# Two unused tiles that shift where a kernel's matmul operands start in on-chip memory

## The chip, the cores and the metric

The kernel runs on one core of one Trainium2 chip. The metric is the device time of one execution in microseconds, given as the median of several runs. Beside it stands one profiled execution, whose trace is read below: PE is the matrix engine (TensorE), PEld its weight loads, DVE the vector engine, ACT the scalar engine, POOL the general engine, SP the engine that issues the DMAs. SBUF is the on-chip memory of 128 partitions, PSUM the memory into which matmuls accumulate.

## The reference

One encoder block in float32 on x of shape (1, 512, 2048): RMSNorm, one input projection, windowed attention beside a chunked gate, one output projection, then a gated MLP with a depthwise convolution of width 3.

```python
z = rmsnorm(x, norm1_g) @ w_in                    # 2048 -> 3584
attn = windowed_gqa(q, k, v, attn_sink)           # 8 heads, 2 kv heads, |t-s| <= 128
gm = chunked_spatial_gating(zg, ...)              # u * (ws @ v + b), 8 groups, chunks of 128
x = x + concat(rmsnorm(attn), rmsnorm(gm)) @ w_out        # 2048 -> 2048
a = rmsnorm(x, norm2_g) @ w_up                    # 2048 -> 11264
g, u = split(conv3(a) + conv_b)
x = x + (silu(g) * u) @ w_down                    # 5632 -> 2048
return rmsnorm(x, final_g)
```

## The kernel before

**Numbers in two halves.** Every matrix operand is held as two float32r tiles, a rounded high part and the remainder. ACT makes the high part (a cast, L76, L89, L446), DVE the remainder (a subtraction, L77, L90, L447). `mm3` (L80 to L83) multiplies two such pairs with three matmuls into one PSUM tile: L81 is high times high, L82 high weights times the low moving part, L83 low weights times the high moving part. In each matmul one operand is *stationary* (128 columns, loaded into PE by an LDWEIGHTS of its own) and the other is *moving* (512 columns as a rule, streamed through PE). There are 8776 of each in the trace; nearly all of the work is 8124 matmuls with 512 moving columns.

**Stages, in order of time.** `g`, `va`, `u` and `vg_ps` are the input projection, with the attention's small matmuls (`sc`, `pt`, `o`) between. `gv` is the chunk gate. `pj` is the output projection, in two halves: in the first the stationary operand is the attention result `atsh`, `atsl`, in the second the gate result `gm..s_h`, `gm..s_l`; the moving operand is in both halves the converted weight `hi_o`, `lo_o`. `up` is the MLP's up-projection (4224 matmuls), interleaved with `dp`, the down-projection in a form with seven block products instead of eight (1680 matmuls, in runs of 12). `dn` is the last group of the down-projection.

**Where the operands lie.** Tiles come from pools, which the framework places one behind the other in SBUF. In order of address: `const` (columns of constants, `ones`, `ident` and others), `big` (64 slots of 2048 bytes a partition: activations `x_h`, `h_h`, `gm..s_h`, `al`, `dl_h`), `tmp`, `small`, then the weight pool `wp`, later `wq` in its place (`st_`, `hi_`, `lo_` tiles of 4096 bytes), and last `oct`, later `raw`, `acp` and `afp` (`atsh`, `afs`, `af`). Since slots and tiles of the larger pools are multiples of 512 bytes, every operand of one pool starts at the same place modulo 256 bytes, which is set by the sizes of the small tiles ahead of it.

**What sets the order.** Each engine runs its own stream in program order, and the framework's semaphores hold an instruction until its operands are ready. Weights are loaded by SP's DMAs of 512 KB, three (front) or six (MLP) tiles ahead.

## Time and profile before

| | |
|---|---|
| median of three runs | 1995.55 us (1995.38 to 1996.44) |
| profiled execution, its own time | 1995.75 us |
| span in its trace, first to last instruction | 1994.0 us |
| PE busy | 1971.3 us, 99% of the span |
| DVE, ACT, POOL busy | 63%, 35%, 3% |
| granted clock of PE, mean | 0.995 of full |

In the trace the duration of a matmul is modelled and longer than the distance to the next one, since matmuls overlap in PE's pipeline. What counts for the time is the distance from one start to the next. The timeline prints starts to 0.01 us, so that distance is best read over many matmuls in a row: last start less first start, over the number of steps.

### The profile page before, as it was taken

How to read it: one execution, taken by the hardware profiler on the slowest of the kernel's cores; microseconds unless marked ns; L12 is line 12 of the kernel's file. 1: busy time of each engine (PE TensorE's matmuls, PEld its weight loads, DVE VectorE, ACT ScalarE, POOL GpSimd, SP SyncE). 2: the span in 40 equal slices, each digit the busy share in tenths (PEclk: the TensorE clock that was granted, in tenths of full speed). 3: DMA queues.
4: the chain of work that ended last, by engine and by line, in shares of the span. 5: the costliest groups of instructions: out<-in, count | busy, mean ns of one | idle time of the engine just before them, and what ended most of it. 6: DMA issues, size and time to landing. Idle time of an engine off the chain costs nothing.

```text
span 1994.0 us, 21954 instructions
## 1 busy us (share of the span) xinstructions
PE 1971.3 (99%) x8776; PEld 1605.1 (80%) x8776; DVE 1261.5 (63%) x1692; ACT 694.6 (35%) x915; POOL 58.1 (3%) x64
## 2 busy tenths in 40 slices
PE   9999999999999999999999999999999999999988
PEld 7887788888878888888888888888888888888866
DVE  7366563434444767667676676667766766758667
ACT  6243442322332333333233342333333333333243
POOL 5001100100000000000000000000000000000000
PEclk9999999999999999999999999999999999999989
DMA  6222232522132222232223322332232222232222
GB/s 219 85 74 66 74 114 85 169 99 91 53 148 84 95 95 95 95 117 85 95 96 115 107 85 96 106 106 95 86 108 103 97 94 104 93 119 85 95 100 102
DMA packets 59575, 201.07 MB, mean 101 GB/s; under 512 B 6864, under 2 KB 7120, under 8 KB 59472
## 3 DMA queue, kind: packets, MB, share of 16 engines
q1 hardware_dynamic: 59472, 199.67, 29.0%
q8 instruction: 68, 1.11, 0.2%
q14 instruction: 35, 0.29, 0.0%
HBM read 195.44 MB, written 4.19 MB: 100 GB/s over the span
## 4 chain that ended last, share of the span: by engine, by line
PE 96%; DVE 1%; issue 1%; DMA 1%; ACT 1%; POOL 0%; SPq 0%; ACTq 0%; DVEq 0%; POOLq 0%
PE up L83 16%; PE up L81 16%; PE up L82 16%; PE dp L82 6%; PE dp L83 6%; PE dp L81 6%; PE pj L81 3%; PE pj L83 3%; PE pj L82 3%; PE u L81 1%; PE vg_ps L83 1%; PE vg_ps L81 1%; PE vg_ps L82 1%; PE u L82 1%; PE u L83 1%; PE g L81 1%
## 5 line engine op out<-in xcount | busy, mean ns | idle before, releaser
L81 PE MATMUL up<-h_h,hi_u 128*128 128x512 f32 x1408 | 555.9, 395 | 2.5 <-ACT hi_u L446 2.5
L83 PE MATMUL up<-h_h,lo_u 128*128 128x512 f32 x1408 | 556.1, 395 | 0.2 <-DVE lo_u L447 0.2
L82 PE MATMUL up<-h_l,hi_u 128*128 128x512 f32 x1408 | 555.4, 394 | 0.0
L81 PEld LDWEIGHTS up<-h_h,hi_u 128*128 128x128 f32 x1408 | 264.4, 188 | 64.5 <-ACT hi_u L446 2.7
L83 PEld LDWEIGHTS up<-h_h,lo_u 128*128 128x128 f32 x1408 | 264.3, 188 | 64.1 <-DVE lo_u L447 0.6
L82 PEld LDWEIGHTS up<-h_l,hi_u 128*128 128x128 f32 x1408 | 264.4, 188 | 63.5
L446 ACT CAST hi_u<-st_u 128x1024 fp32r<-128x1024 f32 x176 | 185.0, 1051 | 323.2 <-PE dp L83 189.4
L447 DVE TENSOR_TENSOR lo_u<-st_u,hi_u 128x1024 fp32r<-128x1024 f32 x176 | 215.0, 1222 | 97.8 <-ACT hi_u L446 97.8
L447 DVE TENSOR_TENSOR lo_b<-st_d,hi_b 128x1024 fp32r<-128x1024 f32 x60 | 73.4, 1223 | 163.0 <-ACT hi_b L446 163.0
L447 DVE TENSOR_TENSOR lo_t<-st_d,hi_t 128x1024 fp32r<-128x1024 f32 x60 | 73.5, 1226 | 126.6 <-ACT hi_t L446 126.6
L545 DVE TENSOR_TENSOR x<-x,dp 128x512 f32<-128x512 f32 x200 | 136.3, 681 | 4.6 <-PE dp L83 2.7
L446 ACT CAST hi_b<-st_d 128x1024 fp32r<-128x1024 f32 x60 | 63.1, 1052 | 193.1 <-PE up L82 193.1
L446 ACT CAST hi_t<-st_d 128x1024 fp32r<-128x1024 f32 x60 | 63.2, 1053 | 174.4 <-PE up L82 174.4
L77 DVE TENSOR_TENSOR lo_i<-st_i,hi_i 128x1024 fp32r<-128x1024 f32 (+1 forms) x57 | 72.8, 1277 | 78.2 <-ACT hi_i L76 78.0
L473 ACT ACTIVATE c<-a,col 128x512 f32<-128x512 f32 x88 | 71.3, 810 | 117.3 <-DVE a L470 117.3
L76 ACT CAST hi_i<-st_i 128x1024 fp32r<-128x1024 f32 (+1 forms) x57 | 58.7, 1031 | 125.4 <-PE u L82 35.6
L77 DVE TENSOR_TENSOR lo_o<-st_o,hi_o 128x1024 fp32r<-128x1024 f32 x32 | 39.2, 1225 | 97.0 <-ACT hi_o L76 97.0
L82 PE MATMUL dp<-lo_t,afs 128*128 128x512 f32 x240 | 93.7, 390 | 0.0
L83 PE MATMUL dp<-hi_t,afs 128*128 128x512 f32 x240 | 93.6, 390 | 0.0
L81 PE MATMUL dp<-hi_t,afs 128*128 128x512 f32 x240 | 93.6, 390 | 0.0
L475 DVE SCALAR_TENSOR_TENSOR c<-a,col,c 128x511 f32<-128x511 f32 x88 | 66.0, 750 | 24.7 <-ACT c L473 24.5
L76 ACT CAST hi_o<-st_o 128x1024 fp32r<-128x1024 f32 x32 | 33.7, 1052 | 115.9 <-PE pj L83 90.6
(278 smaller groups left out, 3210.2 us busy)
## 6 DMA issues: line engine op xcount, KB each, us to landing
st_u<-in_w_up SPq DMA_DIRECT2D x176, 512.0 KB, 3.2
st_d<-in_w_down SPq DMA_DIRECT2D x80, 512.0 KB, 3.2
st_i<-in_w_in SPq DMA_DIRECT2D x55, 512.0 KB, 3.2
st_o<-in_w_out SPq DMA_DIRECT2D x32, 512.0 KB, 3.2
xg<-in_xT SPq DMA_DIRECT2D x16, 256.0 KB, 4.8
x<-in_x SPq DMA_DIRECT2D x16, 256.0 KB, 5.9
st_l<-in_w_down SPq DMA_DIRECT2D x8, 512.0 KB, 3.2
out<-x SPq DMA_DIRECT2D x16, 256.0 KB, 3.0
```

Of the source, the lines that this page charges most:

```text
L76: nc.scalar.copy(hi[:, cs], st[:, cs])
L77: nc.vector.tensor_tensor(lo[:, cs], st[:, cs], f(hi[:, cs]), op=ALU.subtract)
L81: nc.tensor.matmul(ps, a[0], b[0], start=start, stop=False, skip_group_check=free)
L82: nc.tensor.matmul(ps, a[0], b[1], start=False, stop=False, skip_group_check=free)
L83: nc.tensor.matmul(ps, a[1], b[0], start=False, stop=stop, skip_group_check=free)
L446: nc.scalar.copy(hi, st)
L447: nc.vector.tensor_tensor(lo, st, f(hi), op=ALU.subtract)
L473: nc.scalar.activation(t, a, AF.Identity, scale=w[1], bias=col[:, C_CB + j * 44 + i : C_CB + j * 44 + i + 1])
L475: nc.vector.scalar_tensor_tensor(t[:, 1:], a[:, : S - 1], w[0], t[:, 1:], op0=ALU.mult, op1=ALU.add)
L545: nc.vector.tensor_tensor(d, d, ps, op=ALU.add)
```

## The change

Two tiles are allocated that nothing writes or reads: one of 56 float32 (224 bytes a partition) as the first tile of `const`, and one of 16 float32 (64 bytes) in `tmp`, which has two buffers a tile and so grows by 128 bytes.

```diff
+    tmp.tile([P, 16], F32, tag="gap", name="gap")
+    const.tile([P, 56], F32, name="gap0")
     col = const.tile([P, N_COLS], F32, name="col")
     ones = const.tile([P, P], F32, name="ones")
```

The instructions of all five engines, their order and the semaphores that they wait for stay the same; line numbers behind L119 go up by two. What moves is the addresses. In the built programs, the start of each operand modulo 256 bytes is:

| pool | operands | before | after |
|---|---|---|---|
| `const` | `ones`, `ident` | 224 | 192 |
| `big` | `x_h`, `h_h`, `gm..s_h`, `al`, `dl_h`, `vah`, `k_h` | 32 | 0 |
| `wp`, `wq` | `hi_i`, `hi_o`, `hi_u`, `hi_b`, `hi_t` and their `lo_` | 160 | 0 |
| `oct`, `raw`, `afp` | `atsh`, `atsl`, `af`, `afs` | 160 | 0 |

Matmuls of 512 moving columns, by the start of the moving and of the stationary operand before:

| moving | stationary | count | which |
|---|---|---|---|
| 32 | 160 | 5088 | `up` 4224, `g` 480, `u` 384 |
| 160 | 32 | 768 | `vg_ps` 384, `pj` second half 384 |
| 160 | 160 | 2064 | `dp` 1680, `pj` first half 384 |
| 32 | 32 | 204 | `dn` 144, `o` 60 |

So 5856 of the 8124 have their two operands 128 bytes apart modulo 256, and 2268 have them at the same place. After the change all 8124 have both at 0. Of the 256-column matmuls, 192 (`va`) have 160 and 32, and 144 (`dn` 96, `sc` 48) have 32 and 32.

## Rows read from the trace of the kernel before

**Rows 1.** The page: PE's busy time; the chain that ended last, by engine.
```profile
PE 1971.3 (99%) x8776; PEld 1605.1 (80%) x8776; DVE 1261.5 (63%) x1692; ACT 694.6 (35%) x915; POOL 58.1 (3%) x64
...
PE 96%; DVE 1%; issue 1%; DMA 1%; ACT 1%; POOL 0%; SPq 0%; ACTq 0%; DVEq 0%; POOLq 0%
```
**Rows 2.** The page's costliest groups: an up group and a dp group.
```profile
L81 PE MATMUL up<-h_h,hi_u 128*128 128x512 f32 x1408 | 555.9, 395 | 2.5 <-ACT hi_u L446 2.5
...
L82 PE MATMUL dp<-lo_t,afs 128*128 128x512 f32 x240 | 93.7, 390 | 0.0
```
**Rows 3.** Timeline, PE, pj first half: start us, duration us, engine, line, operands.
```profile
376.21 0.39 PE L83 MATMUL pj<-hi_o,atsl 128*128 128x512 f32 x1
...
460.53 0.40 PE L83 MATMUL pj<-hi_o,atsl 128*128 128x512 f32 x1
```
**Rows 4.** Timeline, PE, pj second half.
```profile
480.02 0.40 PE L82 MATMUL pj<-lo_o,gm6s_h 128*128 128x512 f32 x1
...
483.50 0.40 PE L82 MATMUL pj<-lo_o,gm7s_h 128*128 128x512 f32 x1
```
**Rows 5.** Timeline, PE, one unbroken run of up.
```profile
774.56 0.40 PE L81 MATMUL up<-h_h,hi_u 128*128 128x512 f32 x1
...
790.88 0.40 PE L82 MATMUL up<-h_l,hi_u 128*128 128x512 f32 x1
791.12 0.39 PE L83 MATMUL up<-h_h,lo_u 128*128 128x512 f32 x1
```
**Rows 6.** Timeline, PE, one unbroken run of vg_ps.
```profile
209.72 0.40 PE L82 MATMUL vg_ps<-lo_i,x_h 128*128 128x512 f32 x1
...
225.58 0.40 PE L81 MATMUL vg_ps<-hi_i,x_h 128*128 128x512 f32 x1
```
**Rows 7.** Timeline, PE, dn at 512 columns, in the tail.
```profile
1963.85 0.39 PE L81 MATMUL dn<-dl_h,al 128*128 128x512 f32 x1
...
1965.89 0.39 PE L81 MATMUL dn<-dl_h,al 128*128 128x512 f32 x1
```
**Rows 8.** Timeline, PE, one run of 12 dp and the up behind it.
```profile
671.90 0.39 PE L81 MATMUL dp<-hi_t,afs 128*128 128x512 f32 x1
...
672.60 0.39 PE L81 MATMUL dp<-hi_t,afs 128*128 128x512 f32 x1
672.83 0.39 PE L82 MATMUL dp<-lo_t,afs 128*128 128x512 f32 x1
...
674.64 0.40 PE L81 MATMUL up<-h_h,hi_u 128*128 128x512 f32 x1
```
**Rows 9.** Tile va (duration min/median/max ns, first, last start); timeline, dn at 256 columns.
```profile
L81 PE MATMUL va<-hi_i,x_h x64: 279/281/285, 80.1 to 102.5; 128*128 128x256 f32 x64
...
1961.74 0.28 PE L81 MATMUL dn<-dl_h,al 128*128 128x256 f32 x1
...
1962.34 0.28 PE L83 MATMUL dn<-dl_h,al 128*128 128x256 f32 x1
```
**Rows 10.** Timeline, PE, first dn matmuls of the tail.
```profile
1938.37 0.63 PE L81 MATMUL dn<-dl_h,al 128*128 128x512 f32 x1
...
1941.79 0.63 PE L83 MATMUL dn<-dl_h,al 128*128 128x512 f32 x1
```
**Rows 11.** Busy time by stretch: head, MLP, tail.
```profile
core 0: us, PE busy (x) PEld busy (x) DVE busy (x) ACT busy (x) POOL busy (x), PEclk, DMA share, GB/s
0.00:43.00 43.00, 38.60 (x165) 30.77 (x165) 31.66 (x27) 30.16 (x44) 26.90 (x21) 1.00 0.66 230
...
560.00:1930.00 1370.00, 1368.44 (x5912) 1109.12 (x5912) 924.51 (x1119) 463.11 (x519) 0.00 (x0) 1.00 0.29 100
...
1938.00:1942.00 4.00, 4.00 (x11) 3.13 (x10) 2.31 (x4) 4.00 (x9) 0.00 (x0) 0.50 0.65 192
```
**Rows 12.** Waits: waiter <- releaser: us in total, times, longest.
```profile
ACT hi_t L446 <- PE up L82: 225.6, 80, 4.4
...
PE up L81 <- ACT hi_u L446: 2.5, 1, 2.5
```

## The prediction

> **What bounds the kernel now.** I read the page's busy times and its chain of waits first [rows 1]: PE is busy for 99% of the span and carries 96% of the chain that ended last. Then the waits [rows 12]: PE's longest wait in the MLP is a single one of 2.5 us, while ACT waits for PE for hundreds of microseconds, so the conversions run ahead of PE and not behind it. The time is therefore the sum of the distances between matmul starts, and a change that touches no instruction can matter only through those distances.

> The distances are not all alike. The group rows hint at it: a matmul of `up` has a mean duration of 395 ns, one of `dp` 390, at the same shape [rows 2]. Durations are modelled, so I went to starts in the timeline and divided by steps:
> - `pj` first half, operands at 160 and 160: 372 steps in 84.32 us, 226.7 ns each [rows 3].
> - `pj` second half, at 160 and 32: 15 steps in 3.48 us, 232.0 ns [rows 4].
> - `up`, at 32 and 160: 71 steps in 16.56 us, 233.2 ns [rows 5].
> - `vg_ps`, at 160 and 32: 68 steps in 15.86 us, 233.2 ns [rows 6].
> - `dn`, at 32 and 32: 9 steps in 2.04 us, 226.7 ns [rows 7].

> The two halves of `pj` are the cleanest pair: same code, same moving tiles, same PSUM pool; only the stationary tile comes from another pool. The rule that fits all five is that a 512-column matmul takes 226.7 ns where its two operands start at the same place modulo 256 bytes, and some 232 to 233 where they are 128 bytes apart. It holds for both equal places seen (32 and 160) and both unequal orders.

> **The change part by part.** No instruction is added, removed or moved, and no wait; the two tiles hold no data. So the whole effect is the place of operands. The sum is made against the profiled execution's own 1995.75 us (span 1994.0, with 1.75 around it); it lies 0.2 us above the median of the runs, which is nothing.

> *The 5856 unequal matmuls become equal.* The three unequal rows give 232.0, 233.2 and 233.2, mean 232.8; less 226.7 that is 6.1 ns each, and 5856 x 6.1 ns = 35.7 us. `up` alone is 4224 of them, 25.8 us.

> *What of it is lost in the head.* Up to 43 us PE has 165 records and is busy 38.6 of 43 us, since the x tiles and first weights arrive one after the other [rows 11]; a faster matmul there only waits longer. 165 x 6.1 ns = 1.0 us is lost.

> *The run-in of `dp`.* Behind `up`, the first three of a run of 12 take 0.70 us, 233 ns each, and the other nine settle: eight steps in 1.81 us, 226 ns [rows 8]. After the change nothing switches. Read to 0.01 us, the three lose 0.015 to 0.02 us to 3 x 226.7; with 140 runs that is 2.1 to 2.8 us, and I take 2.1.

> *The 192 matmuls of `va` with 256 columns.* They are unequal too, but show no penalty: 63 x 3 steps in 22.4 us, 118.5 ns, against 120.0 ns for the equal `dn` at 256 columns (five steps in 0.60 us) [rows 9]. They may lose 1.5 ns each, 0.3 us.

> *The other engines.* DVE, ACT and the DMAs also read and write shifted tiles. The MLP has room for either sign: DVE is busy 924.5 of 1370 us there and ACT 463.1 [rows 11]. With 30 us less, DVE would be at 69% instead of 67%. I cost this at nothing; the cover is the lead of the conversions [rows 12]. What is late next is again PE itself.

> Sum: 35.7 - 1.0 + 2.1 - 0.3 = 36.5 us, so 1995.75 - 36.5 = 1959.3 us. Its own range is 1955 (6.5 ns a matmul, as in `up`, nothing lost in the head) to 1968 (a quarter lost).

> What the trace doesn't show is any operand at 0. The starts seen, 32 and 160, are alike modulo 128. [...]

> **The rivals.**

> [...]

> *No change: it is the pool and not the place.* Pool and place go together before: each unequal pair takes one operand from `big` and one from `wp`. If crossing those two areas is what costs 6 ns, shifting both changes nothing: 1995.75 us. Against it: `dp` and the first half of `pj` also take their operands from two pools, `wp` and `oct` or `afp`, and are fast. [...]

> *Slower: equal at 0 is a bad equal.* If the moving stream and the weight load of the next matmul, which begin together, meet at the border of a piece when both start at 0, each matmul could pay at every start what `up` now pays on some steps: its last step is 0.24 us [rows 5]. At 240 ns, the 5856 lose 7.2 ns (42 us) and the 2268 lose 13.3 (30 us): 2068 us. It decides from 231.1 ns on, which is today's mean over both kinds ((5856 x 232.8 + 2268 x 226.7) / 8124). For it: nothing shows 0. Against it: two equal places out of two are fast.

> That the change doesn't do what it says I leave out: the built program has every float32r operand at 0.

> **How the numbers follow.** Equal places give 226.7 ns, 1959.3 us: 0.58. Less than that because of the start itself, down to 1849 us: 0.22, with parts of the 13 ns possible. No change: 0.10. Slower: 0.10. The range takes in the first two cases, 1849 to 1968, and leaves 2 in 10 out. A measurement can tell about 0.2% of this kernel, 4 us, from no change; so faster has 0.80, the same 0.10, slower 0.10.

> **What the profile after would show.** Right: `up`, `vg_ps` and the second half of `pj` at 226.7 ns from start to start, the first half of `pj` unchanged, the first three of each `dp` run like the rest, and the MLP's stretch shorter by about 30 us with DVE's and ACT's busy time as before. Wrong in one way: the first half of `pj` below 226.7 ns, down to 214, which is the start itself. Wrong in the other: `up` still at 233 while everything else is as it was, or `dp` above 227.

## The result and the profile after

The changed kernel takes 1960.15 us (median of four runs, 1960.0 to 1961.68) against 1995.99 us before (1995.38 to 1997.01): a ratio of 0.9822, 95% interval 0.9805 to 0.9839. The forecast was 1959.3 us. The profiled execution took 1960.21 us, with a span of 1958.4 us.

The page of the changed kernel, its busy times and two of its groups (line, engine, operands, count; busy us, mean ns; idle before):

```profile
PE 1935.3 (99%) x8776; PEld 1603.8 (82%) x8776; DVE 1255.9 (64%) x1692; ACT 696.2 (36%) x915; POOL 58.0 (3%) x64
...
L81 PE MATMUL up<-h_h,hi_u 128*128 128x512 f32 x1408 | 549.0, 390 | 2.4 <-ACT hi_u L448 2.4
...
L83 PE MATMUL dp<-hi_t,afs 128*128 128x512 f32 x240 | 93.5, 389 | 0.0
```

PE is busy 36 us less, the other engines within 6 us of what they were [rows 1], and the mean of `up` has come down from 395 ns to that of `dp` [rows 2]. PE is still 99% of the span. The starts tell it exactly. Timeline of PE in the changed kernel, in this order: one unbroken run of `up`, one of `vg_ps`, a piece of `pj`'s first half, a piece of its second half, a run of 12 `dp` with the `up` behind it (start us, modelled duration us):

```profile
763.28 0.39 PE L81 MATMUL up<-h_h,hi_u 128*128 128x512 f32 x1
...
779.37 0.39 PE L83 MATMUL up<-h_h,lo_u 128*128 128x512 f32 x1
...
206.94 0.39 PE L82 MATMUL vg_ps<-lo_i,x_h 128*128 128x512 f32 x1
...
222.38 0.39 PE L81 MATMUL vg_ps<-hi_i,x_h 128*128 128x512 f32 x1
...
370.27 0.39 PE L83 MATMUL pj<-hi_o,atsl 128*128 128x512 f32 x1
...
454.58 0.39 PE L83 MATMUL pj<-hi_o,atsl 128*128 128x512 f32 x1
...
472.08 0.39 PE L81 MATMUL pj<-hi_o,gm6s_h 128*128 128x512 f32 x1
...
477.07 0.39 PE L82 MATMUL pj<-lo_o,gm7s_h 128*128 128x512 f32 x1
...
779.60 0.39 PE L81 MATMUL dp<-hi_b,af 128*128 128x512 f32 x1
...
782.32 0.39 PE L81 MATMUL up<-h_h,hi_u 128*128 128x512 f32 x1
```

| stretch | steps | before, ns a step | after, ns a step |
|---|---|---|---|
| `up` | 71 | 233.2 [rows 5] | 16.09 us / 71 = 226.6 |
| `vg_ps` | 68 | 233.2 [rows 6] | 15.44 us / 68 = 227.1 |
| `pj` second half | 15, 22 | 232.0 [rows 4] | 4.99 us / 22 = 226.8 |
| `pj` first half | 372 | 226.7 [rows 3] | 84.31 us / 372 = 226.6 |
| 12 `dp` | 12 | 2.74 us / 12 = 228.3 [rows 8] | 2.72 us / 12 = 226.7 |

What was fast stayed as it was, and what was slow came down to the same 226.7 ns. By stage, from the first start of one to that of the next: the rest of `g` up to `va` gave 2.0 us, `vg_ps` with the attention between 1.3, `u` with `gv` 2.1, `pj`'s first half 0.05, its second half 2.2, and the MLP, from the first `up` to the first `dn`, 27.1 (1375.2 to 1348.1 us). The other stages and the tail make up the rest of the 35.6 us of span.

One thing beside the addresses differs between the two profiled executions: where PE runs at the lower clock. In the MLP's first microseconds the changed kernel had such a stretch, which the kernel before did not have there (PEclk 1.00 from 561 to 568 us). Busy time by stretch (PE busy, PEld, DVE, ACT, POOL, granted clock, DMA share, GB/s) and timeline, changed kernel:

```profile
553.00:560.00 7.00, 6.51 (x21) 4.94 (x22) 5.97 (x16) 2.78 (x4) 0.00 (x0) 0.76 0.96 370
...
555.28 0.63 PE L81 MATMUL up<-h_h,hi_u 128*128 128x512 f32 x1
...
557.84 0.44 PE L81 MATMUL up<-h_h,hi_u 128*128 128x512 f32 x1
```

Behind a wait for the first weights, six steps there went at 427 ns instead of 227; with the slower step on each side of them that is some 1.5 us. So the MLP would have gained some 28.6 us without it. The kernel before had a stretch of the same kind in `g`, which the changed kernel did not have there (PEclk 1.00 from 43 to 49 us). The same two views of the kernel before:

```profile
45.42:48.40 2.98, 2.98 (x8) 2.34 (x7) 2.23 (x10) 0.00 (x0) 0.00 (x0) 0.50 0.76 278
...
45.42 0.63 PE L81 MATMUL g<-x_h,hi_i 128*128 128x512 f32 x1
...
48.41 0.47 PE L82 MATMUL g<-x_l,hi_i 128*128 128x512 f32 x1
```

Seven steps took 2.99 us, 427 ns each, again some 1.5 us too much. So about 1.5 of the 2.0 us that `g` gave come from the clock and not from the addresses, and in the whole time the two stretches cancel. The two single-gap runs below show each of them again, at a granted clock of 0.50: the one with equal starts in `up` (555.45 to 557.57 us), the one with starts 128 apart in `g` (44.84 to 47.80 us).

### The profile page after: what moved, and what is told of

It reads as the page before. It is cut to its first block, busy times and chain, and to the rows that moved or that the text cites. A ratio compares the mean times of both kernels' runs of the same rounds, so it can differ in the third digit from the quotient of the medians.

```text
span 1958.4 us, 21954 instructions
## 1 busy us (share of the span) xinstructions
PE 1935.3 (99%) x8776; PEld 1603.8 (82%) x8776; DVE 1255.9 (64%) x1692; ACT 696.2 (36%) x915; POOL 58.0 (3%) x64
## 4 chain that ended last, share of the span: by engine, by line
PE 96%; DVE 1%; issue 1%; ACT 1%; POOL 0%; DMA 0%; SPq 0%; ACTq 0%; DVEq 0%; POOLq 0%
PE up L83 16%; PE up L81 16%; PE up L82 16%; PE dp L83 6%; PE dp L82 6%; PE dp L81 6%; PE pj L81 3%; PE pj L82 3%; PE pj L83 3%; PE u L81 1%; PE u L83 1%; PE u L82 1%; PE vg_ps L81 1%; PE vg_ps L82 1%; PE vg_ps L83 1%; PE g L83 1%
## 5 line engine op out<-in xcount | busy, mean ns | idle before, releaser
L81 PE MATMUL up<-h_h,hi_u 128*128 128x512 f32 x1408 | 549.0, 390 | 2.4 <-ACT hi_u L448 2.4
L83 PE MATMUL up<-h_h,lo_u 128*128 128x512 f32 x1408 | 549.2, 390 | 0.3 <-DVE lo_u L449 0.3
L82 PE MATMUL up<-h_l,hi_u 128*128 128x512 f32 x1408 | 548.8, 390 | 0.0
```

Source lines behind the costliest of these rows:

```text
L81: nc.tensor.matmul(ps, a[0], b[0], start=start, stop=False, skip_group_check=free)
L82: nc.tensor.matmul(ps, a[0], b[1], start=False, stop=False, skip_group_check=free)
L83: nc.tensor.matmul(ps, a[1], b[0], start=False, stop=stop, skip_group_check=free)
```

## Experiments

### One gap: equal at 32

```diff
     tmp.tile([P, 16], F32, tag="gap", name="gap")
-    const.tile([P, 56], F32, name="gap0")
```

> The gap in `const` is taken out again, the 128 bytes ahead of the weights stay: all float32r operands lie at 32 modulo 256, equal to each other, none at a multiple of 64. Theory (what counts is that the two operands of a matmul start at the same place modulo 256): up, vg_ps and the second half of pj at 226.7 ns from start to start, 1960 us as with both gaps. Rival (what counts is that an operand starts at a multiple of 64, 128 or 256): up stays at 233 ns, 1996 us.

Measured: 1961.8 us (1960.31 to 1962.07), ratio to before 0.983 (0.9813 to 0.9846). One run of 72 `up` in its timeline:

```profile
763.38 0.39 PE L81 MATMUL up<-h_h,hi_u 128*128 128x512 f32 x1
...
779.48 0.39 PE L83 MATMUL up<-h_h,lo_u 128*128 128x512 f32 x1
```

71 steps in 16.10 us, 226.8 ns. Equal at 32 is as good as equal at 0. One tile of 64 bytes, in two buffers, is the whole effect; the gap in `const` adds nothing that these runs can tell.

### The other gap: both at multiples of 128, and apart

```diff
-    tmp.tile([P, 16], F32, tag="gap", name="gap")
     const.tile([P, 56], F32, name="gap0")
```

> The other half: the gap in `const` stays, the one ahead of the weights is taken out. `big` lies at 0, the weights and `oct` at 128 modulo 256: every operand starts at a multiple of 128, but those 5856 matmuls that were 128 bytes apart before are so again. Theory (same place): up at 233 ns, dp at 226.7 behind a run-in of three, 1995 to 1997 us as before. Rival (multiple of 64 or 128): 226.7 ns everywhere, 1960 us. If the start at 0 had taken something off besides: dp, now at 128 and 128, would tell by another spacing than 226.7.

Measured: 1996.23 us (1995.26 to 1997.11), ratio 1.0001 (0.9992 to 1.001). One run of 72 `up`:

```profile
774.64 0.40 PE L81 MATMUL up<-h_h,hi_u 128*128 128x512 f32 x1
...
791.21 0.39 PE L83 MATMUL up<-h_h,lo_u 128*128 128x512 f32 x1
```

16.57 us over 71 steps, 233.4 ns. Every operand starts at a multiple of 128 here, and nothing is gained. Of the starts and distances tried so far, only the distance between the two operands goes with 226.7 or 233 ns; a "well aligned" start alone is worth nothing.

### A table of starts

A kernel of matmuls alone, on slices of two tiles (other rows left out at the dots):

```python
def run(name, a, b, n, count):
    ps = psm.tile([P, S], F32, tag="m", name=name)
    for i in range(count):
        nc.tensor.matmul(ps[:, :n], wt[:, b // 4 : b // 4 + P], mv[:, a // 4 : a // 4 + n],
                         start=i == 0, stop=i == count - 1)
...
for a in range(8):
    for b in range(8):
        run(f"z{L[a]}{L[b]}", 32 * a, 32 * b, S, 96)
...
```

> Not the block: only a scan, nothing of the reference is computed. 96 float32r matmuls with 512 moving columns back to back for each pair of starts, moving at 0, 32 ... 224 and stationary at 0, 32 ... 224 modulo 256 (tiles za.a to zh.h, first letter moving), then eight starts of the stationary operand with 256 columns (y.), then distances of 4 to 16 bytes around 0, 128 and 256 (x.). Theory (only the distance modulo 256 counts): each diagonal of the 8 by 8 table has one value, 226.7 ns at distance 0 and 233 at 128; between them either a step or a slope, which nothing yet tells; the 256-column rows are 118 to 120 ns whatever the start. Rival (each operand's own start counts): rows or columns of the table differ, not diagonals, and (0, 0) lies below (32, 32).

Rows by tile (duration ns min/median/max, first and last start us, shape); the second letter is the moving start, the third the stationary one, a for 0 to h for 224:

```profile
L138 PE MATMUL zaa<-mv,wt x96: 389/389/397, 30.4 to 51.9; 128*128 128x512 f32 x96
...
L138 PE MATMUL zab<-mv,wt x96: 392/395/397, 52.2 to 74.3; 128*128 128x512 f32 x96
...
L138 PE MATMUL zag<-mv,wt x96: 388/392/398, 164.1 to 185.9; 128*128 128x512 f32 x96
...
L138 PE MATMUL zbb<-mv,wt x96: 387/389/397, 230.9 to 252.5; 128*128 128x512 f32 x96
...
L138 PE MATMUL zca<-mv,wt x96: 388/392/397, 386.7 to 408.4; 128*128 128x512 f32 x96
...
L138 PE MATMUL zhh<-mv,wt x96: 389/389/397, 1433.8 to 1455.3; 128*128 128x512 f32 x96
```

Last start less first, over 95 steps, is 226.3 ns for zaa, zhh and 227.4 for zbb (distance 0) by these rounded rows, 232.6 for zab (32), 229.5 for zag and 228.4 for zca (both 192); the rounding to 0.1 us is worth 1 ns a step. From the trace's starts in full the whole table is this, by the stationary start less the moving one, modulo 256; each row holds eight pairs with eight different moving starts:

| distance | ns a step, lowest to highest of eight pairs |
|---|---|
| 0 | 226.7 to 227.0 |
| 32 | 233.3 to 233.3 |
| 64 | 233.3 to 233.4 |
| 96 | 234.2 to 234.3 |
| 128 | 232.3 to 233.4 |
| 160 | 233.3 to 233.4 |
| 192 | 228.9 to 229.0 |
| 224 | 233.3 to 233.4 |

The table has diagonals and, but for one pair at 128 that is 1 ns above the others, nothing else: eight starts at distance 0 agree, and the start itself costs nothing. It is a single run; the last scan below, on another chip, gives the same values at these eight distances to within 1.1 ns. This buries the further 13 ns below the forecast as well as the rival of the bad equal at 0. The distance has a sign (229.0 ns at 192, 233.4 at 64), and the penalty is neither a step nor a slope. No other engine works meanwhile (ACT's last instruction ends at 5.7 us), so no other engine's traffic is needed for the penalty: with the moving operand fixed at 0, moving the weights by 32 bytes alone costs 6.6 ns. With 256 columns the eight distances gave 117 to 120 ns, 0 being among the slowest, so equal places gain nothing there.

### Two distances carried back into the block

The table makes numbers for kernels that were not built yet. Weights at 192 from `big`:

```diff
-    tmp.tile([P, 16], F32, tag="gap", name="gap")
+    tmp.tile([P, 8], F32, tag="gap", name="gap")
```

> The block, complete, with the gap in `const` and 64 instead of 128 bytes ahead of the weights: big at 0, weights at 192. The 5088 matmuls of up, g and u have the stationary operand 192 behind the moving one, the 768 of vg_ps and pj's second half 64. By the scan's table (229.0 ns at 192, 233.4 at 64) they lose 5088 x 2.3 + 768 x 6.7 ns = 17 us, with some 2 us of run-in in dp: 1977 to 1981 us, up at 229.0. Rival (a step: whatever isn't equal costs as much as 128 bytes): 1996 us, up at 233.

and at 96, with a pool of one buffer opened behind `small`, so that 224 bytes stand ahead of the weights (the line that opens it is left out):

```diff
-    tmp.tile([P, 16], F32, tag="gap", name="gap")
+    gapp.tile([P, 56], F32, name="gap")
```

> The block, complete, with the gap in `const` and another one ahead of the weights that puts them at 96: the 5088 matmuls of up, g and u have the stationary operand 96 behind the moving one, the 768 others 160. By the scan's table (234.2 ns at 96, 233.4 at 160) they lose 5088 x 7.5 + 768 x 6.7 ns = 43 us and some 2 us of run-in: 2004 to 2008 us, slower than the kernel before, up at 234.2. Rival (a step): 1996 us, up at 233.

Measured: 1983.83 us at 192 (1982.45 to 1984.83; ratio 0.9937, 0.992 to 0.9953), and 2002.26 us at 96 (2000.39 to 2003.15; ratio 1.0029, 1.0017 to 1.0041): a layout that is slower than the kernel before. Timeline at 192, one run of 72 `up` and the 12 `dp` behind it:

```profile
770.14 0.40 PE L81 MATMUL up<-h_h,hi_u 128*128 128x512 f32 x1
...
786.41 0.39 PE L83 MATMUL up<-h_h,lo_u 128*128 128x512 f32 x1
786.64 0.40 PE L81 MATMUL dp<-hi_b,af 128*128 128x512 f32 x1
...
788.95 0.39 PE L82 MATMUL dp<-lo_b,af 128*128 128x512 f32 x1
...
789.41 0.40 PE L81 MATMUL up<-h_h,hi_u 128*128 128x512 f32 x1
```

and at 96 (where lines are one higher):

```profile
778.33 0.40 PE L82 MATMUL up<-h_h,hi_u 128*128 128x512 f32 x1
...
794.96 0.40 PE L84 MATMUL up<-h_h,lo_u 128*128 128x512 f32 x1
```

`up` takes 16.27 us / 71 = 229.2 ns and 16.63 us / 71 = 234.2 ns, the table's 229.0 and 234.2, so the rival of a step falls. The times are off by 3 us above and 2 us below the expected ranges. At 192 the miss is the run-in: behind `up` it is not three `dp` matmuls that are slow but ten, 2.31 us or 231 ns each from 786.64 to 788.95, and 12 take 2.77 us instead of 2.72. That is 0.05 us x 140 runs = 7 us where I had put 2. At 96, 12 `dp` come out near 227.5 ns on the mean, and the head swallows about 1 us of what the first matmuls lose, as it had swallowed their gain.

### Which weights, which shape, which type, which clock

The rows, in short (a pair alternates from matmul to matmul, comments added; more rows left out):

```python
run("own", (0, 128), (0, 128))       # each matmul equal to its own weights, 128 from the next
run("next", (0, 128), (128, 0))      # the other way round
run("weights", 0, (0, 128)); run("moving", (0, 128), 0)
run("shiftc", 512, 768)
run("colsb", 0, 0, m=64)
run("halfa", 0, 0, x=bm, w=bw, e=2)  # bfloat16; halfe: 0 and 128
...
```

> Not the block: again only rows of 96 matmuls, nothing of the reference is computed. Which of the two weights counts, the matmul's own or the one that is loaded while it streams? Tile own: both operands alternate between 0 and 128 together, so each matmul is equal to its own weights and 128 bytes away from the next ones; tile next: the other way round. Theory A (the load of the next weights meets the running stream): next at 226.7 ns, own at 232 to 233. Rival B (a matmul and its own weights): own at 226.7, next at 232 to 233. Where only one of the two alternates (tiles weights, moving), both say about half the penalty, 229 to 230. Tiles shifta to shiftc: distances of 256 bytes, 226.7 by a period of 256. Tiles cols: 96, 64 and 32 stationary columns at distance 0 and at 128; if the 13.3 ns over 512 columns come from the load, they shrink with its columns, if they are a fixed cost of the exchange they stay. Tiles half: bfloat16 operands at eight distances; if the cost goes by bytes read, the step over 213.3 ns is smaller than 13.3 and the distance matters less. Tile first is at 128 and starts at the low clock: 426.7 ns there means that neither cost shows at that clock.

Rows by tile, with the float32r weight loads of tile `equal` (0 and 0); last, from the page, the group of the bfloat16 weight loads (busy us, mean ns):

```profile
L146 PE MATMUL own<-mv,wt x96: 388/391/396, 51.7 to 73.4; 128*128 128x512 f32 x96
...
L146 PE MATMUL next<-mv,wt x96: 391/392/393, 73.7 to 95.5; 128*128 128x512 f32 x96
...
L146 PE MATMUL weights<-mv,wt x96: 390/393/398, 95.7 to 117.8; 128*128 128x512 f32 x96
...
L146 PE MATMUL moving<-mv,wt x96: 388/392/397, 118.0 to 139.9; 128*128 128x512 f32 x96
...
L146 PE MATMUL shiftc<-mv,wt x96: 389/389/391, 183.7 to 205.2; 128*128 128x512 f32 x96
...
L146 PE MATMUL colsb<-mv,wt x96: 387/391/398, 227.5 to 249.3; 128*64 128x512 f32 x96
...
L146 PE MATMUL halfa<-bm,bw x94: 379/379/389, 316.0 to 336.5; 128*128 128x512 bf16 x94
...
L146 PE MATMUL halfe<-bm,bw x94: 379/379/379, 398.9 to 419.4; 128*128 128x512 bf16 x94
...
L146 PEld LDWEIGHTS equal<-mv,wt x96: 187/188/188, 29.7 to 51.3; 128*128 128x128 f32 x96
...
L146 PEld LDWEIGHTS <-bw 128*128 128x128 bf16 x768 | 75.1, 98 | 90.7 <-issue 0.4
```

- *Own or next: neither.* From the trace's starts in full, `own` takes 228.5 ns a step, `next` 230.0, `weights` 232.2, `moving` 230.0; nothing came out at 226.7, which one of the two theories wanted for `own` or `next`, and `weights` lies above the 229 to 230 that both wanted. That a step can depend on the matmuls before it is also what the run-in of `dp` shows: 233 ns for the first three behind `up`, 226 for the others [rows 8]. Which reads collide with which stays open.
- *A period of 256.* A distance of 256 bytes (`shiftc`) is as good as 0: 21.5 us / 95 = 226.3 ns.
- *Fewer stationary columns don't help.* At distance 0 the step is 230.0 ns with 96 of them, 229.9 with 64 and 231.7 with 32, above the 226.7 of 128. So the 13.3 ns of the expectation (226.7 less 213.4, half of the 426.8 ns that `dn` takes from start to start at a granted clock of 0.50 [rows 10, 11], from its starts in full) do not shrink with the stationary columns; what they are stays open. At distance 128 it is 229.3 ns with 64 columns and 230.7 with 32: with so few, equal places are no longer clearly the better ones.
- *bfloat16 doesn't care.* Two of the 96 records of each of its tiles are missing; over 95 steps it is 20.5 us, 215.8 ns, at distance 0 and at 128 alike, and the same at the six others. But its weight loads differ as well, 98 ns long in the trace against 188 for a float32r one, so these rows change the type and the load together.
- *At the low clock nothing of it shows.* In the kernel before, `g` at distance 128 took 427 ns a step where the granted clock was 0.50 (the stretch from 45.42 us shown above), and so did `dn` at distance 0 in the tail [rows 10, 11]; twice 226.7 would be 453. The first matmuls of this kernel, at distance 128, also start 427 ns apart; its granted clock reads 1.00 there, so that they ran at the low clock is taken from the spacing alone.

### All distances of four bytes

```diff
+    for b in range(64):
+        run(f"u{L[b // 8]}{L[b % 8]}", 0, 4 * b, S, 64)
+    for b in range(63, -1, -1):
+        run(f"d{L[b // 8]}{L[b % 8]}", 0, 4 * b, S, 64)
```

> Not the block: rows of 64 matmuls, nothing of the reference is computed. The moving operand stays at 0, the stationary one goes through all 64 starts of 4 bytes from 0 to 252, once upwards (tiles u..) and once downwards (tiles d..). Theory (the distance decides, 226.7 ns is a floor that no distance undercuts): every value at 226.7 or above, up to some 235, the same in both passes within 1 ns, 0 among the lowest. Rival (another distance is better than 0): some value below 226 ns, which would be a version to build. Second rival (what came before decides, since the pipeline keeps its state): passes differ by several ns at the same start.

Rows by tile; u is the upward pass, d the downward one, and the two letters count the distance in 32 and in 4 bytes:

```profile
L138 PE MATMUL uaa<-mv,wt x64: 389/389/397, 18.9 to 33.2; 128*128 128x512 f32 x64
...
L138 PE MATMUL ueb<-mv,wt x64: 389/389/402, 509.4 to 523.8; 128*128 128x512 f32 x64
...
L138 PE MATMUL ufg<-mv,wt x64: 391/394/398, 702.4 to 717.0; 128*128 128x512 f32 x64
```

Over 63 steps these rounded rows give 227.0 (distance 0), 228.6 (132) and 231.7 ns (184); from the starts in full they are 226.7, 227.5 (which settles to 226.7) and 232.0. Of the 64 distances, four settle at 226.7 in both passes: 0, 120, 132 and 252. Most lie between 229 and 235, about half of all at 233.3. None settles below 226.7, so among these there is no better layout to build. The second rival is right for a part: at eight distances (28, 116, 124, 128, 144, 156, 204, 228) the passes differ by 1 ns or more; 156 gave 226.7 upwards and 244 downwards. Beside 0, then, even a good value may depend on what ran before.

## Why the prediction was right, step by step

- *The rule.* "A 512-column matmul takes 226.7 ns where its two operands start at the same place modulo 256 bytes, and some 232 to 233 where they are 128 bytes apart." It held for a start that the trace did not have, and the single gaps and the scan show that it was the distance and not the start. The scan adds that 128 stands for no general rule: other distances cost anything from nothing to 17 ns.
- *The 5856 matmuls, 35.7 us.* Right in the size: 233.2 to 226.6 in `up`, 233.2 to 227.1 in `vg_ps`. Not all of it reached the time: 384 x 6.1 ns is 2.3 us, and `vg_ps` with the attention's small matmuls between gave 1.3; what took the rest is not shown.
- *The head, 1.0 us lost.* Right, though of the 165 records only 144 are `g`, which makes 0.9: up to the first `r_ps` only 0.3 us were gained (42.9 to 42.6 us), and PE was busy there for as long as before, 38.54 against 38.60 us [rows 11].
- *The run-in, 2.1 us.* Right: 2.74 us for 12 `dp` became 2.72 in the rows shown, and over all 140 runs the mean went from 2.735 to 2.720 us, 2.1 us in all. That the run-in is no constant came out only at 192 bytes, where it was three times as large.
- *`va`, 0.3 us lost.* Right: its matmuls take 22.9 us from the first start to the last, against 22.7 before.
- *The other engines at nothing.* Right: DVE's and ACT's busy times moved by 6 and 2 us, PE's longest wait in the MLP is still one of 2.4 us.
- *The MLP.* 25.8 + 2.1 us were forecast, 27.1 measured, and some 28.6 without the low-clock stretch.
- *The rivals.* The pool instead of the place falls with the change itself, since the pools are the same; in the scan, too, the two tiles stay the same and only the weights' start differs between 226.7 and 233.3 ns, though which reads meet stays open. For bfloat16 it is 215.8 ns at any of eight distances. The start at 0 as a loss falls with the table's diagonal, 226.7 to 227.0 ns at eight starts; the border of a piece in that rival was a supposition, and no run shows one. The 13 ns with which the chances reach down to 1849 us, and the profile to 214 ns, are 226.7 less half of `dn`'s step at a granted clock of 0.50 (427.5 ns by the rounded [rows 10], 426.8 from the starts in full, and so 13.3). That a start at 0 takes them off is a term that no run shows: in its place the first half of `pj` kept its step, 226.7 ns at 160 and 160 [rows 3] and 226.6 at 0 and 0, and the time was 1960.15 us.

What the prediction had by luck is its choice between the forecast and the 13 ns below it: the trace had no operand at 0 that could part them, and 0.22 stood on the wrong one. The table of starts would have settled that beforehand. It is also luck that the sum comes within 1 us of the measured time: it has no term for the clock, and the two low-clock stretches of 1.5 us, one before and one after, happen to cancel.

## What to carry to other kernels

Where the bound is PE and a trace shows two groups of equal shape with different distances from start to start, list early where their operands lie modulo 256 bytes. For float32r matmuls with 512 moving and 128 stationary columns and a weight load each, place the moving and the stationary operand at the same offset modulo 256 (226.7 ns a step here, against 233.3 at about half of the 64 distances); a few bytes in a small pool do it, and a small tile of another size can undo much of it (8 float32 instead of 16 gave 1983.83 us, against 1960.15). The scans show no such gain with 256 moving columns (117 to 120 ns, 0 being among the slowest), with 64 stationary ones (229.9 ns at distance 0, 229.3 at 128), or in bfloat16 (215.8 at both). Measure a layout by starts over many steps, since the page's mean durations show it as 390 against 395.
